# Transformer trunk on one core: opening stage, operand roles in gates and branches, and the planner's urgent calls

## The chip, the cores and the metric

The kernel runs on one core of a Trainium2 chip. A core has five engines that run side by side and meet at semaphores: TensorE (PE in the profile, with its weight loads shown as PEld) multiplies matrices into PSUM, VectorE (DVE) and ScalarE (ACT) work elementwise, GpSimd (POOL) does small side jobs, and SyncE (SP) issues the DMAs that bring data from memory. The metric is the time of one execution on the device in microseconds, the median of several runs.

## The reference

A sequence of 256 tokens of width 1024 passes two layers. Each layer takes shift, scale and gate rows from a vector c through a matrix of 1024 x 6144, normalises the tokens, mixes them by two attention branches that are gated and merged, and then applies a squared-ReLU MLP of width 4096. Cut to what matters:

```python
for l in range(DEPTH):
    ada = c_act @ w_ada[l] + b_ada[l]
    sh1, sc1, gt1, sh2, sc2, gt2 = [a[:, None, :] for a in jnp.split(ada, 6, axis=-1)]
    h = rms(x, g_mix[l]) * (1.0 + sc1) + sh1
    parts = jnp.split(h @ w_in[l], IN_SPLITS, axis=-1)
    y_a = gqa_attention(qa, ka, va) @ w_branch_a[l]
    y_b = dilated_attention(qs, kss, vs) @ w_branch_b[l]
    mixed = sigmoid(gate_a) * y_a + sigmoid(gate_b) * y_b
    x = x + gt1 * (mixed @ w_out[l])
    h2 = rms(x, g_mlp[l]) * (1.0 + sc2) + sh2
    x = x + gt2 * (jnp.square(jax.nn.relu(h2 @ w_ff1[l])) @ w_ff2[l])
```

All data is 32-bit float. Every weight is used once, so some 180 MB pass from memory to the core.

## The kernel before

**Numbers in two parts.** A product of two 32-bit matrices is made of three fast matmuls (`mm3`, line 682): each operand is split into a high part (a rounded copy) and a low part (the rest), and high x high, low x high and high x low are summed in PSUM. The weights come as tiles of 128 x 1024 (512 KB, `wr`); ACT writes the high part and DVE the low part (`split_next`, line 661). The activations are split the same way after each normalisation (`make_h`, line 731, into the tiles `hT`) and after each attention branch.

**Stages.** First c is made into `c_act`, spread over all partitions by small matmuls against columns of the identity. DVE multiplies each 128 x 1024 tile of the modulation matrix with it and sums along the row (`ada_tile`, line 597): 96 such tiles in all, 16 of which must be done before layer 0 has its first shift and scale. The opening loop (line 1320) takes one k block of 128 features at a time: two modulation tiles, the scaled and split activations of that block, and two weight tiles for four of the six QKV chunks. Ahead of it three matmuls on zeros (`WARM`) run. Then per layer follow the rest of the QKV chunks, the norm and rotary steps, attention a in four steps of head pairs and b in two, eight units of gate, four of branch a and four of branch b, the output product in two halves of 128 tokens, the residual and the norm for the MLP, and the MLP (`mlp`, line 1157). `CFG["seq0"]` and `CFG["seq1"]` give the order in which these pieces are written down: c a chunk, u and v a gate unit, a and b an attention step, w one modulation tile, y a piece of branch a.

**Which operand moves.** TensorE holds one operand of 128 x 128 (stationary) and passes the other through it (moving). In the QKV chunks, the output product and the second MLP product the activations are stationary and 512 weight columns move, so the result has tokens on the partitions. In `gates`, `ya` and the branch b loop the weights are stationary and the 256 tokens move (`wide`, line 1027), so the result has features on the partitions, as the output product needs its stationary operand `mT`:

```python
def wide(ps, i, wh, wl, xs, nk):
    o = ps[:, i * S : (i + 1) * S]
    for k in range(nk):
        mm3(o, wh[:, k, :], wl[:, k, :], *xs.parts(k, slice(0, S)), k == 0, k == nk - 1)
```

**The order of the work.** Nothing is issued as it is written. `Plan` (line 130) records each call with an estimated occupancy and latency (`cost`), links the calls by the data they share, gives each a due time from the place of the TensorE calls that need it (`due`), and plays the whole kernel against a clock (`run`): each engine takes the ready call that is due first, where its buffers fit (eight PSUM banks, seven short work tiles, fourteen large tiles, six raw weight tiles). `run` is repeated four times, each fed with the start times of the last, and the order of the shortest becomes the program: five queues, fixed before the chip starts. A call already lets an engine stay idle for a short time where another one due much earlier is nearly ready (`patience`). DMAs inside `plan.first()` go to the front of SP's queue.

**The point before the MLP.** The output product runs for tokens 0 to 127, then 128 to 255 (`mixer`, line 1081). After each half follow, on DVE, ACT and POOL, `residual`, `sum_sq`, the power on POOL, the scaling, eight transposes on TensorE and `make_h`. The first MLP unit (`ff1_first`, line 1168) needs the result of its half of the tokens.

Of the kernel before, what the change touches and what calls it, by code (L numbers as in the profile page):

```python
# [35 lines left out]
  dve_ss=0, hk=2,  # L36
# [5 lines left out]
WARM = 3  # L42
PSCALE = "aa"
PASSES = 4
HOLD = 400

# [83 lines left out]
class Plan:  # L130


    def __init__(self, tc, pools):
# [7 lines left out]
        self.soon = False  # L141
# [34 lines left out]
    @contextmanager  # L176
    def first(self):

        self.soon = True
        yield  # L180
        self.soon = False

# [34 lines left out]
    def record(self, e, op, a, k):  # L217
# [11 lines left out]
        o["occ"] += self.hold  # L229
        from_sbuf = all(z.space == bass.MemoryType.SB for z in ins)  # L230
# [4 lines left out]
    def cost(e, op, outs, ins, k):  # L235
# [3 lines left out]
        if e == "PE":  # L239
# [7 lines left out]
            occ = 232 if n > 256 else 119 if n > 128 else 109  # L247
# [3 lines left out]
        if e == "POOL":  # L251
            occ = 400 + 150 * n if k.get("op") == ALU.pow else 440 + 1.7 * n
            return occ, occ + 60
# [114 lines left out]
    def run(self, due):  # L368
# [8 lines left out]
        pipe = [1500.0]  # L377
# [11 lines left out]
        seen = dict.fromkeys(ORDERED)  # L389

        def fits(i):
# [14 lines left out]
            return True  # L406

# [5 lines left out]
        while count < n:  # L413
            moved = False
            for e in ORDERED:
# [15 lines left out]
                if pick is None and seen[e] == state[0]:  # L431
                    continue
                held = []
# [11 lines left out]
                if pick is not None and e != "SP" and not forced:  # L445

                    end = t + ops[pick]["occ"]
                    for r, j in w:
                        if r < end and due[j] < due[pick] - self.patience and (r - t) < 0.5 * ops[pick]["occ"] and fits(j):
                            held.append((due[pick], pick))  # L450
                            pick = None
                            break
                for h in held:
                    heapq.heappush(q, h)
# [23 lines left out]
                if e == "SP":  # L478
                    b = max(pipe[0], t + 2100.0) + o["lat"] / 380.0
                    pipe[0] = b  # L480
                    end = b + 1600.0
# [73 lines left out]
def encoder(ctx: ExitStack, tc: tile.TileContext, a: dict, out: bass.AP):  # L555
# [23 lines left out]
    def f32(t):  # L579
        return t.bitcast(F32)  # L580


    x = cp.tile([P, 2, D], F32, name="x")
    consts = cp.tile([P, P + 96 + 32 + 8], F32, name="consts")
    ident, small = consts[:, :P], consts[:, P:]
# [19 lines left out]
    def sh_sc(l, w, k0, k1):  # L605
# [5 lines left out]
        )  # L611

# [19 lines left out]
    def ada_jobs():  # L632
        for l in range(DEPTH):
            for w in range(2):
                shg[l, w] = tl("sbuf", [P, 2, KT], F32, "shg", 3, f"shg{l}{w}")
                for k in range(KT):
                    for s in range(2):
                        ada_tile(l, w, s, k, shg[l, w][:, s, k : k + 1])
                        if s == 1 and (l, w) == (0, 0):
                            sh_sc(0, 0, k, k + 1)  # L640
# [46 lines left out]

    ss_of = {}

    def sum_sq(l, w, t, c):  # L690
# [5 lines left out]
        if CFG["dve_ss"]:  # L696
# [4 lines left out]
    def rms_x(l, w, t):  # L701
# [5 lines left out]
        for g in range(2):  # L707
            xn = s2k(f"xn{l}{w}{t}{g}")
            dve.tensor_scalar(xn, x[:, t, g * 512 : (g + 1) * 512], r, None, op0=ALU.mult)
# [21 lines left out]
    def make_h(l, w, t, hT):  # L731
        v = shg[l, w]
        for g, ps in enumerate(rms_x(l, w, t)):
            h = s2k(f"h{l}{w}{t}{g}")
            for k in range(4):
                kk = 4 * g + k
                o, i = h[:, k * P : (k + 1) * P], ps[:, k * P : (k + 1) * P]
                if k < CFG["hk"]:
# [5 lines left out]
            dve.tensor_copy(hi, hv)  # L744
# [3 lines left out]
    def first_tables():  # L748
# [4 lines left out]
        gc = small[:, 128:136]  # L753
# [4 lines left out]
        for s in range(8):  # L758
            act.activation(dg[:, s * HD : (s + 1) * HD], e, AF.Copy, scale=gc[:, s : s + 1])
# [122 lines left out]
    def qkv_chunk(l, c, hT, T):  # L882
        pss = [pb(f"qkv{l}_{c}_{t}") for t in range(2)]
        for j in range(4):
            wh, wl = weights_k(2)
            for t in range(2):
                for k in range(2):
                    kk = 2 * j + k
                    lh, ll = hT.parts(kk, slice(t * P, (t + 1) * P))
                    mm3(pss[t], lh, ll, wh[:, k, :], wl[:, k, :], kk == 0, kk == KT - 1)  # L890
# [151 lines left out]
    def gates(l, hT, G, u, bank):  # L1042
        if u % 4 == 0:
# [411 lines left out]
```

## Time and profile before

| quantity | value |
| --- | --- |
| median of 3 runs | 755.84 us (755.43 to 757.5) |
| span of the profiled execution, first to last instruction | 754.0 us |
| TensorE busy, matmuls | 739.9 us in 4246 matmuls |
| VectorE, ScalarE, GpSimd busy | 595.4, 470.7, 70.2 us |
| read from memory | 178.66 MB, 238 GB/s over the span |
| mean granted TensorE clock | 0.995 |

The profile records one execution; its own time is its span with the start and end of a launch around it, which the records do not show, and the timed runs lie 1.4 to 3.5 us above the span. Almost every instruction carries line 551, at which the planner issues the calls, so its groups are to be told apart by the tiles they write and read: `ps<-w,hT` is a matmul that moves weights through stationary activations, `ps<-hT,w` one that moves activations, `ps<-consts,s2k` a transpose (the identity moves). A matmul's listed duration reaches beyond the start of the next one, since matmuls are pipelined; the time that one costs is the distance between the starts.

### The profile page before, as it was taken

The page shows a single profiled execution, that of the slowest core. Times are in us where ns is not written, and L with a number is a line of the kernel's source. Part 1 is how long each engine was busy: PE and PEld are TensorE (multiplying, and loading weights), DVE is VectorE, ACT ScalarE, POOL GpSimd, SP SyncE. Part 2 cuts the span into 40 slices and gives each one's busy share as a digit, 9 for nine tenths or more (in the row PEclk, how much of TensorE's full clock was granted, in tenths as well). Part 3 has the DMA queues.
Part 4 walks back from the last instruction along what each step waited for, and adds up shares of the span by engine and source line. Part 5 has one row for each costly group of instructions (what it writes and reads, how often), then busy time and mean ns, then how long its engine had stood idle before and what let it go on. Part 6 is the DMA issues. An engine that isn't in the chain of part 4 may idle for free.

```text
span 754.0 us, 11447 instructions
## 1 busy us (share of the span) xinstructions
PE 739.9 (98%) x4246; PEld 629.9 (84%) x4246; DVE 595.4 (79%) x905; ACT 470.7 (62%) x784; POOL 70.2 (9%) x60
## 2 busy tenths in 40 slices
PE   7999999999999999999999999999998999999997
PEld 4888898998788888888888788889987888888886
DVE  5999999889899989566499899778879976556633
ACT  8668469785558766655256557599535865555630
POOL 0007840000000060000002111000000000000000
PEclk9999999999999999999999999999999999999999
DMA  8996379976579999666145566966635986656201
GB/s 336 385 401 208 128 246 330 356 261 234 178 283 370 386 355 341 248 223 222 58 155 182 219 242 236 363 198 212 235 140 184 344 305 224 204 191 219 88 29 56
DMA packets 50391, 180.47 MB, mean 239 GB/s; under 512 B 5624, under 2 KB 6048, under 8 KB 50336
## 3 DMA queue, kind: packets, MB, share of 16 engines
q1 hardware_dynamic: 50336, 179.75, 66.6%
q8 instruction: 33, 0.54, 0.3%
q14 instruction: 22, 0.18, 0.1%
HBM read 178.66 MB, written 1.06 MB: 238 GB/s over the span
## 4 chain that ended last, share of the span: by engine, by line
PE 84%; DVE 7%; issue 4%; ACT 3%; DMA 1%; POOL 1%; SPq 0%; POOLq 0%; ACTq 0%; DVEq 0%
PE ps L551 84%; DVE s2k L551 4%; DVE w L551 2%; ACT s2k L551 2%; DVE rstd L551 1%; DMA x<-in_x 1%; ACT pr L551 1%; ACT w L551 0%; POOL s2k L551 0%; DVE x L551 0%; DVE hT L551 0%; ACT xT L551 0%; SPq L551 0%; POOL ss L551 0%; ACT c_act L551 0%
## 5 line engine op out<-in xcount | busy, mean ns | idle before, releaser
L551 DVE TENSOR_TENSOR w<-wr,w 128x1024 fp32r<-128x1024 f32 x236 | 288.0, 1238 | 61.0 <-ACT w L551 60.6
L551 ACT ACTIVATE w<-wr 128x1024 fp32r<-128x1024 f32 x236 | 245.6, 1058 | 87.2 <-PE ps L551 48.0
L551 PE MATMUL ps<-hT,w 128*128 128x256 f32 (+1 forms) x1664 | 263.8, 315 | 0.0
L551 PEld LDWEIGHTS ps<-hT,w 128*128 128x128 f32 x1664 | 234.4, 190 | 23.6 <-issue 2.6
L551 PE MATMUL ps<-w,r2k 128*128 128x512 f32 (+1 forms) x792 | 178.8, 385 | 0.0
L551 PEld LDWEIGHTS ps<-w,r2k 128*128 128x128 f32 x792 | 144.4, 188 | 30.1
L551 PE MATMUL ps<-w,hT 128*128 128x512 f32 x672 | 163.3, 399 | 5.0 <-DVE hT L551 2.7
L551 PEld LDWEIGHTS ps<-w,hT 128*128 128x128 f32 x672 | 126.2, 191 | 33.8 <-DVE hT L551 4.5
L551 DVE CUSTOM_DVE_ANT_0 s2k<-wr,c_act 128x1024 bf16<-128x1024 f32 x96 | 117.7, 1240 | 2.3 <-DMA wr<-in_w_ada 1.6
L551 ACT ACTIVATE s2k<-ps 128x512 f32<-128x512 f32 (+3 forms) x136 | 61.5, 479 | 64.0 <-PE ps L551 55.0
L551 PE MATMUL ps<-w,mT 128*128 128x512 f32 x192 | 44.5, 391 | 0.0
L551 ACT ACTIVATE s2k<-s2k 128x512 f32<-128x512 f32 (+1 forms) x62 | 38.3, 620 | 6.0 <-DVE s2k L551 5.2
L551 PEld LDWEIGHTS ps<-w,mT 128*128 128x128 f32 x192 | 35.8, 188 | 7.3
L551 POOL TENSOR_TENSOR rstd<-rstd,half 128x8 f32<-128x8 f32 (+1 forms) x20 | 35.7, 1795 | 61.7 <-DVE rstd L551 61.7
L551 DVE TENSOR_TENSOR s2k<-ps,s2k 128x256 f32<-128x256 f32 x56 | 23.6, 421 | 17.1 <-ACT s2k L551 17.1
L551 ACT ACTIVATE pr<-pr,st 128x256 f32<-128x256 f32 (+1 forms) x64 | 35.7, 614 | 0.6 <-DVE st L551 0.6
L551 POOL TENSOR_TENSOR ss<-ss,half 128x1 f32<-128x1 f32 x8 | 4.4, 554 | 312.2 <-DVE ss L551 312.2
L551 DVE TENSOR_TENSOR r2k<-s2k,r2k 128x512 fp32r<-128x512 f32 x28 | 19.6, 699 | 15.6 <-ACT r2k L551 15.6
L551 ACT ACTIVATE s2k<-x 128x512 bf16<-128x512 f32 x16 | 10.0, 627 | 31.2 <-DVE x L551 28.3
L551 DVE TENSOR_TENSOR s2k<-ps,gtb 128x512 f32<-128x512 f32 (+1 forms) x18 | 11.8, 659 | 20.5 <-PE ps L551 18.7
L551 PE MATMUL ps<-oa,w 128*128 128x256 f32 x192 | 26.1, 288 | 0.0
L551 PE MATMUL ps<-consts,s2k 128*128 128x128 f32 x148 | 22.6, 281 | 2.9 <-DVE s2k L551 2.4
(82 smaller groups left out, 498.1 us busy)
## 6 DMA issues: line engine op xcount, KB each, us to landing
wr<-in_w_ff SPq DMA_DIRECT2D x120, 512.0 KB, 5.2
wr<-in_w_ada SPq DMA_DIRECT2D x96, 512.0 KB, 5.3
wr<-in_w_gate SPq DMA_DIRECT2D x32, 512.0 KB, 5.1
wr<-in_w_qkv SPq DMA_DIRECT2D x24, 512.0 KB, 4.6
wr<-in_w_x SPq DMA_DIRECT2D x16, 512.0 KB, 3.2
wr<-in_w_out SPq DMA_DIRECT2D x16, 512.0 KB, 5.4
wr<-in_w_y SPq DMA_DIRECT2D x8, 512.0 KB, 5.5
wr<-in_w_ba SPq DMA_DIRECT2D x8, 512.0 KB, 4.9
```

Of the source, the lines that this page charges most:

```text
L551: getattr(self.real[o["e"]], o["op"])(*map(real, o["a"]), **{n: real(z) for n, z in o["k"].items()})
```

## The change

The diff does six things.

1. The opening. The constants come inside the two transfers of x and no longer in one of their own, the columns that spread c come with c, one warm-up matmul stays of three, the first two modulation tiles are asked for ahead of the table, sums of squares are shared by ACT and DVE, the diagonal for the rotary table is one DVE instruction, and the first k block's activations are made in halves.
2. `gates`, `ya` and branch b hold the activations and move 512 weight columns. Their results have tokens on the partitions, so branch b's merged result is transposed by TensorE before it is split into `mT`. A gate group takes two PSUM banks over four weight tiles.
3. `many` puts the products with the low part of the weights behind those with the high part, in the opening, the QKV chunks and the second MLP product; `ff1_first` puts those with the low part of the activations last.
4. `make_h` gives the first four feature blocks to ACT and the other four to DVE.
5. The planner's durations are new numbers, for matmuls, POOL and DMA.
6. Calls inside `plan.rush` are marked, on DVE and ACT, and before an engine takes an unmarked call the planner asks whether one of the next marked ones will be ready before that call ends (`called`); if so the engine is left idle.

```diff
-WARM = 3
+WARM = 1
+DEEP = 3
+URGE = 500.0
+GIVE = 0.75
...
+        o["rush"] = self.urgent and e in ("DVE", "ACT")
...
-            occ = 232 if n > 256 else 119 if n > 128 else 109
+            occ = 228.5 if n > 256 else 120.5 if n > 128 else 109
...
+        def called(e, pick, end):
+
+            q = rushed[e]
+            while q and start[q[0]] is not None:
+                q.pop(0)
+            for j in q[:4]:
+                if start[j] is None and due[j] < due[pick] - URGE:
+                    z = expect(j)
+                    if t + 1.0 < z < end and z - t < GIVE * (end - t):
+                        return True
+            return False
...
+                    if pick is not None and rushed[e] and not ops[pick]["rush"] and called(e, pick, end):
+                        held.append((due[pick], pick))
+                        pick = None
...
-                    b = max(pipe[0], t + 2100.0) + o["lat"] / 380.0
+                    quiet = t < 4000.0
+                    b = max(pipe[0], t + (1200.0 if quiet else 2100.0)) + o["lat"] / 400.0
...
+    def many(jobs):
+
+        for ps, lh, ll, rh, rl, start, stop in jobs:
+            pe.matmul(ps, lh, rh, start=start, stop=False)
+            pe.matmul(ps, ll, rh, start=False, stop=False)
+        for ps, lh, ll, rh, rl, start, stop in jobs:
+            pe.matmul(ps, lh, rl, start=False, stop=stop)
...
-                if k < CFG["hk"]:
+                if g == 0:
                     act.activation(o, i, AF.Identity, bias=v[:, 0, kk : kk + 1], scale=v[:, 1, kk : kk + 1])
...
-            dve.tensor_copy(hi, hv)
+            for k0 in (0, 2):
+                if g == 0:
+                    act.activation(hi[:, k0 : k0 + 2], hv[:, k0 : k0 + 2], AF.Copy)
+                elif k0 == 0:
+                    dve.tensor_copy(hi, hv)
...
-    def gates(l, hT, G, u, bank):
...
+    def gates(l, hT, G, pss, u):
+        g, part = divmod(u, 2)
...
+        if part == 0:
+            pss[:] = [pb(f"g{l}_{g}_{t}") for t in range(2)]
+        for j in (2 * part, 2 * part + 1):
+            wh, wl = weights_k(2)
+            for t in range(2):
+                for k in range(2):
+                    kk = 2 * j + k
+                    lh, ll = hT.parts(kk, slice(t * P, (t + 1) * P))
+                    mm3(pss[t], lh, ll, wh[:, k, :], wl[:, k, :], kk == 0, kk == KT - 1)
...
+        wb = [weights_k(2) for _ in range(2)]
+        for t in range(2):
+            ts = slice(t * P, (t + 1) * P)
+            for c in range(2):
...
+                m = s2k(f"yb{l}_{t}{c}s")
+                dve.tensor_tensor(m, ps, G[1][:, t, cs], op=ALU.mult)
+                dve.tensor_tensor(m, m, M[:, t, cs], op=ALU.add)
+                tp = pt(f"mT{l}_{t}{c}")
+                for k in range(4):
+                    pe.transpose(tp[:, k * P : (k + 1) * P], m[:, k * P : (k + 1) * P], ident)
...
+            with plan.rush(t == 1):
+                for c in range(2):
+                    residual(l, 0, t, c, ps[c])
+                    sum_sq(l, 1, t, c)
+                make_h(l, 1, t, h2)
...
+                for lows in range(2):
+                    for kk in range(KT):
+                        lh, ll = h2.parts(kk, slice(t * P, (t + 1) * P))
+                        wh, wl = (z[:, kk % 2, :] for z in ws[kk // 2])
+                        if lows:
+                            pe.matmul(ps, ll, wh, start=False, stop=kk == KT - 1)
+                        else:
+                            pe.matmul(ps, lh, wh, start=kk == 0, stop=False)
+                            pe.matmul(ps, lh, wl, start=False, stop=False)
...
     with plan.first():
-        sp.dma_start(c_row, a["c"])
-        sp.dma_start(x[:, 0, :], a["x"][0])
-        sp.dma_start(consts, a["consts"])
-        sp.dma_start(x[:, 1, :], a["x"][1])
+        sp.dma_start(c_in, a["c"])
+        for t in range(2):
+            sp.dma_start(xin[:, t, :], a["x"][t])
...
-                ps[:, k * P : (k + 1) * P], ident[:KT, kk : kk + 1].to_broadcast([KT, P]), c_row,
+                ps[:, k * P : (k + 1) * P], pick[:, kk : kk + 1].to_broadcast([KT, P]), c_row,
...
-            sum_sq(0, 0, t, c)
+            sum_sq(0, 0, t, c, c == 1)
...
-    tabs_of[0] = first_tables()
+    with plan.first():
+        ada(2)
+        tabs_of[0] = first_tables()
...
+        if k == 0:
+            for t in range(2):
+                ts = slice(t * P, (t + 1) * P)
+                dve.tensor_scalar(h[:, ts], xT[:, k, ts], v[:, 1, k : k + 1], v[:, 0, k : k + 1], op0=ALU.mult, op1=ALU.add)
+                act.activation(hi[:, ts], h[:, ts], AF.Copy)
+                dve.tensor_tensor(lo[:, ts], h[:, ts], f32(hi[:, ts]), op=ALU.subtract)
...
-        for pair in ((0, 1), (2, 5)):
+        for pair in ((0, 1), (2, 5)) if k < KT - 1 else ((2, 5), (0, 1)):
```

More of the change, by code (lines that the diff above doesn't have):

```diff
@@ L181, in first, with rush @@
         self.soon = False
+    @contextmanager
+    def rush(self, on=True):
+        self.urgent = on
+        yield
+        self.urgent = False
     @contextmanager
@@ L406, in fits, with expect @@
             return True
+        rushed = {e: [o["i"] for o in ops if o["e"] == e and o["rush"]] for e in ORDERED}
+        def expect(i, depth=0):
+            z = 0.0
+            for j, how in ops[i]["need"].items():
+                if start[j] is not None:
+                    b = start[j]
+                elif depth < DEEP:
+                    b = expect(j, depth + 1)
+                else:
+                    return 1e18
+                z = max(z, b + (ops[j]["lat"] if how == 2 else ops[j]["occ"]))
+                if z > 1e17:
+                    break
+            return max(z, t)
+        def called(e, pick, end):
[8 more added lines that the diff above has]
+            return False
         for o in ops:
@@ L430, in run @@
                     seen[e] = None
-                if pick is None and seen[e] == state[0]:
+                if pick is None and seen[e] == state[0] and e not in again:
                     continue
+                if e in again:
+                    again.remove(e)
                 held = []
@@ L1205, in ff1, with ff2_job @@
             return hid
+        def ff2_job(hid, w, j, i, t, c):
+            lh, ll = (z[:, (i % 2) * S + t * P : (i % 2) * S + (t + 1) * P] for z in hid[i // 2])
+            wh, wl = (z[:, c * 512 : (c + 1) * 512] for z in w)
+            last = 5 if (l, t, c) == (DEPTH - 1, 1, 1) else 7
+            return accs[2 * t + c], lh, ll, wh, wl, j == 0 and i == 0, j == last and i == 3
         def ff2_one(hid, w, j, i, t, c):
@@ L1222, in mlp @@
                     w = weights()
-                    for t in range(2):
-                        for c in range(2):
-                            ff2_one(hids[j - 1], w, j - 1, i, t, c)
+                    many([ff2_job(hids[j - 1], w, j - 1, i, t, c) for t in range(2) for c in range(2)])
         if l == 0:
@@ L1284, in encoder @@
         layer_weights(l)
[L1285 removed]
+    c_in = cp.tile([KT, P + KT], F32, name="c_in")
+    c_row, pick = c_in[:, :P], c_in[:, P:]
     with plan.first():
[L1287 to L1290 removed]
+        sp.dma_start(c_in, a["c"])
+        for t in range(2):
+            sp.dma_start(xin[:, t, :], a["x"][t])
     c_sig = s2k("c_sig")[:KT, :P]
```

180 lines of the change are left out of this document (103 added, 77 removed).

## The prediction

> **What bounds the kernel now.** I began with the page's busy shares and its chain of waits.
>
> ```profile
> PE 739.9 (98%) x4246; PEld 629.9 (84%) x4246; DVE 595.4 (79%) x905; ACT 470.7 (62%) x784; POOL 70.2 (9%) x60
> ...
> PE 84%; DVE 7%; issue 4%; ACT 3%; DMA 1%; POOL 1%; SPq 0%; POOLq 0%; ACTq 0%; DVEq 0%
> ```
>
> TensorE (PE) is busy nearly all the time and carries 84% of the chain. So the time is the opening, before PE has real work, plus the matmuls' own time, plus small gaps. The waits say what PE waited for (total us, times, longest us):
>
> ```profile
> PEld ps L551 <- DVE hT L551: 4.5, 5, 1.9
> ...
> PE ps L551 <- DVE hT L551: 2.7, 4, 1.4
> ...
> PE ps L551 <- ACT w L551: 0.2, 1, 0.2
> ```
>
> Its waits are for the transposed activations hT, hardly ever for a split weight w: 0.2 us in the whole run. A table of stretches (busy us of each engine, granted clock, DMA share, GB/s) shows what lies close behind:
>
> ```profile
> 15.90:19.30 3.40, 3.40 (x10) 2.48 (x9) 3.40 (x7) 3.40 (x6) 0.00 (x0) 0.50 1.02 404
> ...
> 20.00:60.00 40.00, 40.00 (x178) 33.12 (x177) 37.46 (x63) 25.29 (x34) 0.09 (x1) 1.00 1.02 391
> 60.00:220.00 160.00, 157.82 (x1089) 137.94 (x1088) 149.68 (x248) 112.29 (x213) 39.11 (x32) 1.00 0.69 238
> 300.00:380.00 80.00, 80.00 (x400) 67.47 (x399) 47.45 (x64) 42.41 (x63) 0.55 (x1) 1.00 0.54 184
> ...
> 575.70:579.10 3.40, 3.40 (x10) 2.82 (x11) 3.33 (x7) 1.83 (x4) 0.00 (x0) 0.50 0.05 19
> ```
>
> VectorE (DVE) has 37.46 of 40 us at 20 to 60 and 149.68 of 160 us at 60 to 220, about 94%, but only 59% at 300 to 380. DMA is full at 20 to 60. Twice PE had half its clock for 3.4 us, which costs 1.7 us each time.
>
> **The opening.** The rows, in order of time (start, length, engine):
>
> ```profile
> 1.45 4.93 PE L551 MATMUL ps<-warm 128*128 128x512 f32 x6 [1.45 <-DVE half L551]
> ...
> 2.59 0.28 DVE L551 SCALAR_TENSOR_TENSOR c_row<-s2k,c_row 8x128 f32<-8x128 f32 x1 [1.17 <-ACT s2k L551]
> ...
> 6.31 2.05 PE L551 MATMUL ps<-c_row,consts 8*128 8x128 f32 x16
> ...
> 7.41 0.63 ACT L551 ACTIVATE s2k<-x 128x512 bf16<-128x512 f32 x1 [0.82 <-DMA x<-in_x]
> ...
> 9.84 1.06 ACT L551 ACTIVATE c_act<-ps 128x512 f32<-128x512 f32 x2
> ...
> 10.93 1.23 DVE L551 CUSTOM_DVE_ANT_0 s2k<-wr,c_act 128x1024 bf16<-128x1024 f32 x1 [0.45 <-ACT c_act L551]
> ...
> 12.70 2.02 ACT L551 ACTIVATE w<-wr 128x1024 fp32r<-128x1024 f32 x2
> ...
> 14.60 0.62 ACT L551 ACTIVATE hT<-xT,shg 128x256 fp32r<-128x256 f32 x1
> ...
> 15.27 8.95 PE L551 MATMUL ps<-w,hT 128*128 128x512 f32 x31 [2.27 <-ACT hT L551]
> ```
>
> The row c_row is ready at 2.87, but PE is in the warm matmuls until 6.38, so it spreads c at 6.31 to 8.36; ScalarE (ACT) copies it at 9.84, after the squares of x and eight small diagonal copies; only then, at 10.93, does DVE start the first modulation sum. The change takes two of three warm matmuls away (1.64 us each, 4.93/3), brings the 8 by 8 picker with c so that the spreading no longer waits for the constants, and makes the diagonal one DVE instruction. Then c is spread from about 3.1. If that runs at half clock, 2.05 becomes 4.1 us and c_act is ready near 8 instead of 10.9. On SP's queue the order becomes c, x, x, two modulation tiles, rope table, weights: one issue fewer (the constants ride on x, same bytes), the table behind the tiles. In 0 to 12.5 us DMA moved about 300 GB/s (3.7 MB), and the first weight tile is complete after 3.0 MB, near 10.5 to 11.5, so it can be split by about 12.5. The two sums from 8.5 (1.23 us each), 0.3 us of small sums and the new quarter-size h take until about 11.8 to 12.5. PE then starts at about 12.8 instead of 15.27: -2.5 us. What could take it back is the pace after it. One k needs 24 matmuls of 0.227 us (row below), 5.45 us, against four tiles of 512 KB at 391 GB/s, 5.36 us. From the first weight 29 more tiles and the mask, 15.5 MB, take 39.6 us, to about 51.6; with the last split and matmuls the stage can end near 56.6, against 15.27 + 1.7 + 8 x 5.45 = 60.6 before. So DMA allows at most 4.0 us. Bounds: 0 (DVE, at 94%, gives nothing back) to -4.0. That the half-clock stretch stays (1.7 us) I keep; if fewer warm matmuls bring a second one, the gain falls to 0.8. DVE also gets two sums of squares and gives two scalings to ACT; both lie ahead of the modulation sums, in time that DVE waits.
>
> **Gates and branches with weights moving.** Before, weights stand in the array and 256 columns of activations move; after, activations stand and 512 weight columns move, so half as many matmuls of twice the width. Rows of unbroken stretches:
>
> ```profile
> 177.23 15.84 PE L551 MATMUL ps<-w,mT 128*128 128x512 f32 x69
> 192.91 1.03 PE L551 MATMUL ps<-consts,s2k 128*128 128x128 f32 x8
> 193.70 6.42 PE L551 MATMUL ps<-w,mT 128*128 128x512 f32 x27
> 199.95 4.70 PE L551 MATMUL ps<-w,hT 128*128 128x512 f32 x20
> ```
>
> ```profile
> 529.58 8.80 PE L551 MATMUL ps<-oa,w 128*128 128x256 f32 x72
> 538.22 5.82 PE L551 MATMUL ps<-ob,w 128*128 128x256 f32 x48
> 543.87 8.36 PE L551 MATMUL ps<-w,mT 128*128 128x512 f32 x36
> ```
>
> From start to start: (538.22 - 529.58)/72 = 120.0 ns at 256 columns, 5.65/48 = 117.7 for ob, and 15.68/69 = 227.2 at 512. The code counts 768 such matmuls in the gates of both layers, 192 in branch a, 96 in branch b: 960 x 120.0 + 96 x 117.7 ns = 126.5 us. After: 528 x 227.2 = 120.0. Saved 6.5 us. New are 32 transposes, four to a unit of branch b (two halves of tokens by two of columns, two layers): eight took 0.79 us (192.91 to 193.70), 99 ns each, and the stretch behind them took 6.25 us against 27 x 0.2272 = 6.13, so 0.12 for the switch: 8 x (4 x 0.099 + 0.12) = +4.1 us. Net -2.4 us. All of it is PE's own, with nothing to hide it; bounds -3.3 (no switch) to -1.5 (two).
>
> The Trainium skill, "TensorE: Matmul & The Clock Gate", section "Wait — 56ns, not 53.3ns?", speaks against this: it gives a fixed cost of only about 2.5 ns a matmul. By that an estimate of 528 pairs saves 1.3 us, and the transposes make the edit a loss of 2.8. The rows here give 2 x 120.0 - 227.2 = 12.8 ns, five times that; I go by the rows.
>
> The weights come in tiles of the same size, each for 12 matmuls of 227 ns (2.73 us) in place of 24 of 120 (2.88), so DMA and DVE get the same work in slightly less time. DVE has 10.3 us free of the 160 at 60 to 220, enough for the 1.2 us there. What changes is PSUM: a gate group holds two of eight banks over four tiles (10.9 us) where one bank was held over two (5.8). Nothing in this trace shows a shortage; the nearest is a gap while PE waited for a softmax:
>
> ```profile
> 96.31 0.33 PE L551 MATMUL ps<-consts,pr 128*128 128x128 f32 x1 [0.74 <-ACT pr L551]
> ```
>
> I charge one more such gap: +0.9 us with its small change, bounds -2.2 (all PE idle time of 60 to 220 gone, 160 - 157.82, by the better order) to the slow rival below.
>
> **The urgent calls.** Before the MLP the second half of the tokens must pass residual, norm, transposes and split while PE has little left:
>
> ```profile
> 565.60 2.35 DVE L551 TENSOR_TENSOR w<-wr,w 128x1024 fp32r<-128x1024 f32 x2
> ...
> 567.87 0.68 DVE L551 TENSOR_TENSOR s2k<-ps,gtb 128x512 f32<-128x512 f32 x1
> ...
> 569.19 1.22 DVE L551 TENSOR_TENSOR w<-wr,w 128x1024 fp32r<-128x1024 f32 x1
> ...
> 572.55 0.95 PE L551 MATMUL ps<-w,hT 128*128 128x512 f32 x3
> ...
> 574.95 0.50 PE L551 MATMUL ps<-w,hT 128*128 128x512 f32 x1 [1.45 <-DVE hT L551]
> ...
> 575.67 1.65 PE L551 MATMUL ps<-w,hT 128*128 128x512 f32 x3 [0.23 <-DVE hT L551]
> ```
>
> PE idles from 572.55 + 3 x 0.227 = 573.23 to 574.95 (1.72) and again 0.49 for the low half; then comes the half clock, 1.7 us. Two weight splits held DVE until 567.95; the output matmuls ended before the next ones began at 566.56, so the residual stood about 1.2 us behind splits nobody needed yet, and the split at 569.19 cost 0.3 more. The change reserves DVE and ACT for just these calls and computes both products with the high half first, which hides the second gap (0.49). Saved 1.2 + 0.3 + 0.49 = 2.0 of 2.2, and with a near-whole load the half clock should not follow. The moved copy of the first half costs ACT two instructions in place of one on DVE, inside ACT's idle time. I take -3.2 us (bounds 0 to -3.9). Queued behind the reserved engine are weight splits, which PE would wait for; it now waits 0.2 us for them. The same place in layer 0:
>
> ```profile
> 205.28 1.17 PE L551 MATMUL ps<-w,hT 128*128 128x512 f32 x4
> 207.21 0.49 PE L551 MATMUL ps<-w,hT 128*128 128x512 f32 x1 [0.77 <-DVE hT L551]
> 207.94 0.73 PE L551 MATMUL ps<-w,hT 128*128 128x512 f32 x2 [0.23 <-DVE hT L551]
> ```
>
> Gaps of 1.02 and 0.50 us, no half clock: -1.0 (bounds 0 to -1.5). The regrouped products in the QKV chunks and the MLP issue the same matmuls in another order, each with its own weight load: 0. The planner's new lengths only reorder; they sit in the +0.9.
>
> **Sum.** -2.5 - 2.4 - 3.2 - 1.0 + 0.9 = -8.2 us. The profiled span is 754.0, which makes 745.8; the median of the runs shown is 755.84, 1.8 us above that span, and nothing in the change touches what lies around it: 747.6 us.
>
> **Rivals.** (a) More: the opening reaches DMA's limit (-1.5 more) and the idle 2.2 us at 60 to 220 go as well in place of the +0.9: 747.6 - 1.5 - 3.1 = 743.0. For it: those gaps are waits for order, not for capacity. Against: DVE at 94%. (b) The reservation does not do what it says, because the planner's clock is not the chip's: the half clock and most of the gaps stay, +4.2: 751.8. For it: the delay was only 1.5 us long. Against: the high-first order works without it. (c) Halving the count saves nothing, each wide matmul taking as long as the two that it replaces: +6.5, 754.1; the cadence rows of mT, oa and ob speak against it. (By the section named above an estimate would stand 1.3 us below that.) (d) Slower: PSUM. In each of the 12 attention steps (four and two in each layer) PE must find other matmuls under the softmax:
>
> ```profile
> 484.24 2.34 ACT pr L551 x9
> ```
>
> If the banks held by gate groups leave it none for half of that, 1.17 us, the loss is 14.0 us: 761.6. It decides from 8.2/12 = 0.7 us a step. Against: gates are themselves the filler, and almost all of today's softmaxes are covered.
>
> **Chances.** Forecast 0.50, (a) 0.15, (b) 0.20, (c) 0.05, (d) 0.10. A change within 0.3% (2.3 us) can't be told from none, so (b) is mostly faster, and (c) is no change. Faster 0.82, same 0.08, slower 0.10. The range reaches from (a) to past (c): 742.5 to 755.0; the forecast's own is 744.5 to 750.5.
>
> **What would show it.** The first 512-wide matmul near 12.8; c_act copied before 9; 1056 matmuls of 256 columns replaced by 528 of 512, at 227 ns; 32 more transposes; no half-clock stretch near 570 and gaps under 0.7 us there; PE's idle time at 60 to 220 under 4 us. Wrong would be a start after 14.5, new PE waits for ACT pr, DVE w or a bank in the gate stages, or transposes that leave PE waiting for mT.

## The result

| | before | changed | ratio, 95% interval |
| --- | --- | --- | --- |
| first comparison | 755.84 us (754.96 to 757.68) | 752.28 us (751.13 to 754.12) | 0.9950 (0.9933 to 0.9967) |
| second comparison | 756.15 us (754.41 to 758.23) | 753.37 us (752.02 to 753.79) | 0.9955 (0.9938 to 0.9972) |
| span of the profiled execution | 754.0 us | 749.4 us, in the second comparison 752.0 us | |

The change makes the kernel 2.8 to 3.6 us faster, less than half of the 8.2 us that were forecast. The page of the changed kernel has 500 matmuls fewer and VectorE and ScalarE about as busy as before:

```profile
PE 738.6 (99%) x3746; PEld 600.4 (80%) x3746; DVE 594.1 (79%) x906; ACT 472.5 (63%) x786; POOL 69.2 (9%) x60
...
PE 83%; DVE 8%; ACT 4%; DMA 3%; issue 2%; POOL 1%; ACTq 0%; DVEq 0%
```

The chain of waits still runs 83% over TensorE; VectorE's share went from 7 to 8%, DMA's from 1 to 3%. TensorE's busy time fell by only 1.3 us where the span fell by 4.6: a matmul's record reaches past the start of the next one, so short waits vanish in it, and for costs I use distances between starts. The waits (us in all, times, longest) say where the new gaps lie:

```profile
PE ps L600 <- DVE w L600: 1.1, 3, 0.6
...
PE ps L600 <- ACT w L600: 0.4, 1, 0.4
PE ps L600 <- ACT hT L600: 0.2, 1, 0.2
```

Before, TensorE waited 2.7 us for DVE hT and next to nothing for a split weight. Now hT is down to 0.2 us, and 1.5 us are waits for a split weight, beside 1.4 us for DVE s2k (2.4 before). The stretches (busy us of PE, PEld, DVE, ACT and POOL, then the granted clock, the DMA share and GB/s):

```profile
15.27:18.70 3.43, 3.43 (x17) 2.84 (x16) 3.43 (x5) 3.43 (x6) 0.00 (x0) 1.00 1.02 391
60.00:220.00 160.00, 157.45 (x834) 122.20 (x834) 148.22 (x241) 112.31 (x216) 37.92 (x30) 1.00 0.69 240
571.00:578.00 7.00, 6.59 (x30) 4.85 (x30) 6.71 (x13) 5.23 (x12) 0.00 (x0) 1.00 0.44 129
```

The half-clock stretches of the opening and of layer 1's entry are gone: the clock is 1.00 where it was 0.50 at 15.9 and at 575.7. But at 60 to 220, where half as many matmuls of twice the width should have given TensorE time back, it idles 2.55 us where it idled 2.18.

**The timeline** of the changed kernel, first the opening, then two of the gaps in layer 0, unbroken rows of wide matmuls in layer 1, and the entry to layer 1's MLP (start, length, engine):

```profile
1.49 2.07 PE L600 MATMUL ps<-warm 128*128 128x512 f32 x2 [1.49 <-DVE warm L600]
...
3.49 3.78 PE L600 MATMUL ps<-c_in 8*128 8x128 f32 x16
...
5.60 0.60 ACT L600 ACTIVATE c_act<-ps 128x512 f32<-128x512 f32 x1
...
6.53 0.69 DVE L600 CUSTOM_DVE_ANT_0 s2k<-xin 128x512 bf16<-128x512 f32 x1 [0.75 <-DMA xin<-in_x]
...
7.30 0.60 ACT L600 ACTIVATE c_act<-ps 128x512 f32<-128x512 f32 x1 [1.11 <-PE ps L600]
...
8.54 0.16 DVE L600 SCALAR_TENSOR_TENSOR ss<-ss 128x1 f32<-128x1 f32 x1 [0.92 <-ACT s2k L600]
...
9.01 0.69 DVE L600 TENSOR_TENSOR s2k<-s2k,xin 128x512 f32<-128x512 f32 x1
...
9.62 1.22 DVE L600 CUSTOM_DVE_ANT_0 s2k<-wr,c_act 128x1024 bf16<-128x1024 f32 x1
...
11.36 2.08 PE L600 MATMUL ps<-s2k,s2k 64*128 64x128 f32 x8
...
13.37 0.89 PE L600 MATMUL ps<-xin,s2k 128*128 128x128 f32 x4
...
14.20 1.14 PE L600 MATMUL ps<-s2k,s2k 64*128 64x128 f32 x8
...
15.27 44.94 PE L600 MATMUL ps<-w,hT 128*128 128x512 f32 x194
...
121.67 1.22 DVE L600 CUSTOM_DVE_ANT_0 s2k<-wr,c_act 128x1024 bf16<-128x1024 f32 x1
...
122.82 1.22 DVE L600 TENSOR_TENSOR w<-wr,w 128x1024 fp32r<-128x1024 f32 x1
...
124.09 0.73 PE L600 MATMUL ps<-w,hT 128*128 128x512 f32 x2 [0.60 <-DVE w L600]
...
129.38 0.73 PE L600 MATMUL ps<-w,hT 128*128 128x512 f32 x2 [0.40 <-ACT w L600]
...
444.69 13.99 PE L600 MATMUL ps<-w,hT 128*128 128x512 f32 x61
458.57 0.66 PE L600 MATMUL ps<-xin,s2k 128*128 128x128 f32 x4
...
527.14 8.32 PE L600 MATMUL ps<-w,oa 128*128 128x512 f32 x36
535.30 3.67 PE L600 MATMUL ps<-w,ob 128*128 128x512 f32 x15
...
565.76 0.69 DVE L600 TENSOR_TENSOR s2k<-ps,gtb 128x512 f32<-128x512 f32 x1
...
570.75 1.18 PE L600 MATMUL ps<-w,hT 128*128 128x512 f32 x4
572.17 1.20 PE L600 MATMUL ps<-w,hT 128*128 128x512 f32 x4 [0.25 <-ACT hT L600]
```

c is spread and copied much earlier, but the first wide matmul starts at 15.27, as before (14.91 in the second profile). At 124.09 TensorE waits for a split weight that VectorE could begin only at 122.82, behind a modulation sum. At 572.17 the entry to the MLP has a gap of 0.25 us where there were 1.72 and 0.49.

**By stages.** Five events, taken from the timeline of each kernel, cut the span: the start of the 192nd wide matmul (end of the opening), of the last output matmul of layer 0 (`ps<-w,mT`), of the first matmul on `r2k` in layer 0 (the MLP has been entered), of the last output matmul of layer 1, and of its first matmul on `r2k`. Lengths in us:

| kernel | opening | L0 mixing | L0 entry to MLP | L0 MLP and L1 mixing | L1 entry to MLP | rest | span |
| --- | --- | --- | --- | --- | --- | --- | --- |
| before | 60.3 | 139.4 | 25.6 | 341.0 | 28.3 | 159.4 | 754.0 |
| changed | 59.4 | 141.7 | 24.7 | 339.4 | 25.0 | 159.2 | 749.4 |
| changed, second profile | 58.8 | 143.1 | 24.7 | 340.4 | 25.1 | 159.7 | 752.0 |
| old roles | 58.5 | 143.4 | 25.8 | 340.7 | 25.1 | 159.7 | 753.3 |
| new roles alone | 60.2 | 139.8 | 25.6 | 343.4 | 28.4 | 159.8 | 757.2 |
| no urgent marks | 59.3 | 142.9 | 24.7 | 339.9 | 25.1 | 159.7 | 751.6 |
| low part in old order | 59.5 | 142.4 | 25.9 | 340.7 | 26.4 | 159.8 | 754.6 |
| old lengths in the plan | 60.3 | 143.8 | 24.5 | 342.6 | 24.5 | 159.2 | 754.8 |
| late tables | 59.1 | 144.2 | 25.5 | 340.6 | 25.1 | 159.8 | 754.3 |
| scaling of three chunks on ACT | 58.7 | 140.5 | 25.3 | 339.7 | 25.0 | 159.2 | 748.5 |
| scaling of two chunks on ACT | 59.0 | 139.0 | 25.3 | 339.7 | 25.0 | 159.2 | 747.2 |
| the same, second profile | 59.3 | 139.8 | 25.5 | 340.0 | 25.1 | 159.8 | 749.3 |

The two profiles of the changed kernel show how far to trust such a table: a mixing stage repeats within 1.0 to 1.4 us, the two entries within 0.2. Each row is one execution, whose time lies up to 1.5 us from the median of its kernel (the changed kernel's first row 1.1 below it, old roles 1.5 below, low part in old order 1.3 above). Against before, the changed kernel gains 3.2 to 3.3 us at layer 1's entry, 0.9 at layer 0's, 0.6 to 1.6 in layer 1's mixing and 1.0 to 1.5 in the opening, and loses 2.3 to 3.7 us in layer 0's mixing. That loss is what the experiments had to explain.

### The profile page after: what moved, and what is told of

Its sections match the earlier page's. It is cut to its first block, busy times and chain, and to the rows that moved or that the text cites. A ratio compares the mean times of both kernels' runs of the same rounds, so it can differ in the third digit from the quotient of the medians.

```text
span 749.4 us, 10437 instructions
## 1 busy us (share of the span) xinstructions
PE 738.6 (99%) x3746; PEld 600.4 (80%) x3746; DVE 594.1 (79%) x906; ACT 472.5 (63%) x786; POOL 69.2 (9%) x60
## 4 chain that ended last, share of the span: by engine, by line
PE 83%; DVE 8%; ACT 4%; DMA 3%; issue 2%; POOL 1%; ACTq 0%; DVEq 0%
PE ps L600 83%; DVE s2k L600 3%; DVE w L600 2%; ACT s2k L600 2%; DMA wr<-in_w_ada 1%; DMA wr<-in_w_qkv 1%; ACT w L600 1%; DMA wr<-in_w_x 1%; DMA wr<-in_w_gate 1%; DVE rstd L600 1%; ACT pr L600 1%; POOL rstd L600 1%; DVE st L600 0%; DVE pr L600 0%; ACT G L600 0%
## 5 line engine op out<-in xcount | busy, mean ns | idle before, releaser
L600 PE MATMUL ps<-w,hT 128*128 128x512 f32 x1056 | 260.1, 397 | 1.8 <-DVE w L600 1.1
L600 PEld LDWEIGHTS ps<-w,hT 128*128 128x128 f32 x1056 | 193.9, 188 | 48.4 <-issue 4.5
L600 PE MATMUL ps<-hT,w 128*128 128x512 f32 (+1 forms) x896 | 159.5, 338 | 0.0
L600 PEld LDWEIGHTS ps<-hT,w 128*128 128x128 f32 x896 | 138.0, 188 | 20.2
L600 POOL TENSOR_TENSOR rstd<-rstd,half 128x8 f32<-128x8 f32 (+1 forms) x20 | 33.4, 1678 | 61.0 <-DVE rstd L600 60.9
L600 PEld LDWEIGHTS ps<-xin,s2k 128*128 128x128 f32 x180 | 22.0, 147 | 13.0 <-DVE s2k L600 3.9
L600 PE MATMUL ps<-xin,s2k 128*128 128x128 f32 x180 | 28.7, 288 | 3.2 <-DVE s2k L600 1.4
L600 ACT ACTIVATE s2k<-xin 128x512 bf16<-128x512 f32 x14 | 8.7, 624 | 28.0 <-DVE xin L600 25.9
```

Source lines behind the costliest of these rows:

```text
L600: getattr(self.real[o["e"]], o["op"])(*map(real, o["a"]), **{n: real(z) for n, z in o["k"].items()})
```

## The experiments

Theory S says that VectorE, and not TensorE, sets the length of layer 0 up to its last output matmul; what TensorE saves there, or how early it starts, cannot show. The rivals are that the new operand roles starve TensorE of PSUM banks or weights, that the urgent marks hold VectorE or ScalarE back, and that the plan is simply a fragile one (theory or rival O in the expectations). Each expectation names what it sets against each other; each run is timed against the kernel before on the same chip.

**Part 2 undone.** Gates and branches get their old roles, all else as changed:

```diff
-                    mm3(pss[t], lh, ll, wh[:, k, :], wl[:, k, :], kk == 0, kk == KT - 1)
...
+            wide(ps, i, wh, wl, hT, KT)
...
-                    mm3(yps[t], lh, ll, wh[:, k, :], wl[:, k, :], kk == 0, kk == 3)
...
+                wide(ps, i, wh[:, :, i * P : (i + 1) * P], wl[:, :, i * P : (i + 1) * P], T["oa"], 4)
```

> The changed kernel with part 2 undone: gates and both branches hold the weights again, no transposes of the merged result; all else as changed (752.28 us). Theory S (shared load): layer 0's mixing stage is held by VectorE and DMA, so the 1.2 us that TensorE saves there shows up as waits, and only layer 1's 1.2 us is worth anything: 753.5 us, and TensorE's new gaps at 120 to 140 us (2.7 us) go away. Theory O (order): the gaps are an accident of the planned order, the saving itself is whole: without both, 752.28 + 2.4 - 2.7 = 752.0 us. If the prediction's term was right and nothing else hangs on it: 754.7 us.

756.54 us, ratio 1.0004 (0.9986 to 1.0021): the whole gain is gone, and the time lies above all three that were expected. By stages, though, layer 0's mixing is as long with the old roles (143.4) as with the new ones (141.7 and 143.1). So the new roles did not lengthen it, and nothing shows that they shortened it. The profiled execution is the fastest of ten, so its row shows only a part of the loss.

**Part 2 alone**, put into the kernel before (the same edit, the other way round).

> The kernel before (755.84 us) with part 2 alone: weights move in gates and branches, 32 transposes more. By the cadences 2.4 us of TensorE time go. Theory S: layer 0's half of it is eaten by waits there, 754.6 us. Theory O: all of it shows, 753.4 us, unless this order has gaps of its own. Matmuls: 528 fewer, in both.

758.99 us, ratio 1.0026 (1.0008 to 1.0044): a small loss, where both theories expected a gain. Layer 0's mixing keeps its length (139.8 against 139.4). Layer 1's mixing, where the saving should show, is 2.4 us longer, with new gaps (TensorE idles 4.9 us in it in place of 2.3); one row of the timeline of this kernel:

```profile
510.36 1.21 PE L551 MATMUL ps<-w,oa 128*128 128x512 f32 x4 [0.80 <-DVE st L551]
```

A branch group starts late by 0.80 us, released when VectorE had read scores out of PSUM. That looks like the bank shortage of the prediction's rival (d), on a small scale. In the changed kernel, where the roles come with new lengths and order, this gap isn't there; with the old lengths in the plan it is back (0.80 us at 512.45). So the roles gain with the rest and lose alone; the two numbers don't add.

**The marks off.**

```diff
-        o["rush"] = self.urgent and e in ("DVE", "ACT")
+        o["rush"] = False
```

> The changed kernel with no call marked as urgent; all else as changed (752.28 us). If the reservation made the gain ahead of the MLP, the residual of the second half stands behind weight splits again: 1.5 us in layer 1 and, with the half-clock stretch, 3.2 us, and some 0.5 in layer 0: 756.0 us. Rival: the order of the low-part products and the shared split of the activations made it, the marking is worth nothing: 752.3 us, no half-clock stretch near 570 us.

753.40 us, ratio 0.9952 (0.9934 to 0.9970), the same as the changed kernel, with the same entries to the MLP (24.7 and 25.1 us). The reservation is worth nothing, and does no harm.

**The low part in its old order** at the entry to the MLP:

```diff
-                        if lows:
-                            pe.matmul(ps, ll, wh, start=False, stop=kk == KT - 1)
-                        else:
-                            pe.matmul(ps, lh, wh, start=kk == 0, stop=False)
-                            pe.matmul(ps, lh, wl, start=False, stop=False)
...
+                    mm3(ps, lh, ll, wh, wl, kk == 0, kk == KT - 1)
```

> The changed kernel with the first MLP unit's products in the old order (high, low, cross per block); the marks stay. If putting the low-part products last made the gain ahead of the MLP: layer 1's gap and half-clock stretch come back, 3.3 us, and 1.0 us in layer 0: 756.6 us. If the shared split of the activations in the norm step made it: 752.3 us.

755.06 us, ratio 0.9987 (0.9972 to 1.0001). Layer 1's entry is 1.3 to 1.5 us longer, layer 0's 1.2. Its timeline:

```profile
575.33 0.50 PE L600 MATMUL ps<-w,hT 128*128 128x512 f32 x1 [0.18 <-ACT hT L600]
576.70 0.66 PE L600 MATMUL ps<-xin,s2k 128*128 128x128 f32 x4 [0.87 <-ACT s2k L600]
577.73 2.60 PE L600 MATMUL ps<-w,hT 128*128 128x512 f32 x10 [0.37 <-DVE hT L600]
```

Three gaps come back (0.18, 0.87, 0.37), and no half clock after them. So of the 3.3 us at layer 1's entry about 1.4 is this order; that the half clock stays away (1.7 us) hangs on neither the order nor the marks by itself; both undone together weren't run. The time lies between the two expected (756.6 and 752.3).

**Late tables.** The products for the rotary table and the last transposes of x are put behind the first twelve wide matmuls:

```diff
-        tabs_of[0] = first_tables()
+        tab_parts = first_tables()
+        tabs_of[0] = tab_parts[0]
...
+            if k == 0 and pair == (0, 1):
+                x_copy(*next(x_parts))
+                first_tables_rest(*tab_parts)
```

> The changed kernel with TensorE's rotary table products and the last four transposes of x placed behind the first 12 wide matmuls instead of ahead of them. Theory: TensorE's own queue held the start at 15.27 us while the first operands were ready at 13.7: the start moves to about 13.8 us and the whole to 750.8 us. Rival: VectorE and DMA pace the opening (VectorE 94% busy, DMA full), the start moves but the 192nd wide matmul stays at 59.4 us: 752.3 us.

755.03 us, ratio 0.9976 (0.9959 to 0.9992). TensorE starts 1.2 to 1.6 us earlier, and nothing comes of it; by the medians the kernel is even 1.6 us slower than the one without marks (753.40) on the same chip, and slower than either expectation:

```profile
13.70 3.29 PE L600 MATMUL ps<-w,hT 128*128 128x512 f32 x13
16.92 1.14 PE L600 MATMUL ps<-s2k,s2k 64*128 64x128 f32 x8
```

The opening ends at 59.1, within the spread of the changed kernel (58.8 to 59.4), since the work put off is done in it all the same, and the last output matmul of layer 0 comes at 203.3, with 185.1 us of VectorE's work ahead of it. The start of the first wide matmul, which I had taken as the measure of the opening, doesn't set its end.

**VectorE's load, less and more.** In the first of these two runs seven of the eight modulation tiles of layer 0's first gate are left out, and the gate is zero there, so that part of layer 0 isn't computed; in the second eight sums are done twice:

```diff
-                    ada_tile(l, w, 2, k, gcol[l, w][:, k : k + 1])
+                    if (l, w) != (0, 0) or k == 0:
+                        ada_tile(l, w, 2, k, gcol[l, w][:, k : k + 1])
```

> The changed kernel without seven of the eight modulation tiles of layer 0's first gate row (their columns are set to zero, so layer 0's gate is left out in part): 7 x 1.31 us of VectorE work and 3.7 MB of transfers fewer in layer 0's mixing stage, no TensorE work touched. Theory S (VectorE holds this stage): the stage from the 192nd wide matmul to the last output matmul, 141.7 us, shrinks until TensorE's own gaps there (6.3 us of 60 to 160) are down to some 2, to 137 us; 748 us in all. Rival O (gaps are accidents of the order): 141 to 142 us and about 752 us.

```diff
-        dve.tensor_tensor_reduce(junk, raw, c_act, 0.5, 0.0, ALU.mult, ALU.add, col)
+        for _ in range(2 if (l, w, s) == (0, 0, 2) else 1):
+            dve.tensor_tensor_reduce(junk, raw, c_act, 0.5, 0.0, ALU.mult, ALU.add, col)
```

> The changed kernel with each of those eight modulation sums done twice into the same column: 8 x 1.31 = 10.5 us more of VectorE work in layer 0's mixing stage, no transfer and no TensorE work more. Theory S: nearly all of it shows, the stage grows from 141.7 to about 150 us, 761 us in all. Rival O, with VectorE's 10.6 idle us in that stage to take it: at most 3 us more. If transfers and not VectorE held the stage: no change.

746.37 us, ratio 0.9886 (0.9844 to 0.9929), and 762.84 us, ratio 1.0104 (1.0057 to 1.0151). These two speak for theory S. The stretch from the start to layer 0's last output matmul in one row each (length, then busy us of PE, PEld, DVE): the kernel before,

```profile
0.00:199.72 199.72, 194.63 (x1232) 165.32 (x1233) 180.35 (x303) 142.23 (x261) 39.95 (x37) 0.99 0.78 283
```

the changed kernel,

```profile
0.00:201.06 201.06, 196.10 (x980) 151.10 (x981) 181.79 (x309) 140.99 (x254) 40.88 (x37) 1.00 0.78 281
```

the new roles alone,

```profile
0.00:200.06 200.06, 194.75 (x985) 150.35 (x985) 179.87 (x303) 142.09 (x260) 38.20 (x37) 0.99 0.77 282
```

fewer sums,

```profile
0.00:194.02 194.02, 191.69 (x980) 151.66 (x981) 174.71 (x298) 139.29 (x254) 38.16 (x37) 1.00 0.76 275
```

and more sums:

```profile
0.00:212.33 212.33, 198.85 (x981) 153.03 (x982) 190.08 (x323) 140.75 (x253) 39.75 (x37) 0.98 0.73 264
```

VectorE's busy time goes from 174.7 over 180.4 and 181.8 to 190.1, the end of the stage from 194.0 over 199.7 and 201.1 to 212.3. The difference between the two, VectorE's idle time, is 19.3, 19.4, 19.3 and 22.2 us. TensorE's 250 matmuls fewer (1232 to 980 records) move nothing. Fewer sums also leave out 3.7 MB of DMA (7 x 512 KB), so that run alone would not decide; but the doubled sums, which move no byte more, lengthen the stretch by 11.3 us for 8.3 us more of VectorE's work. The 3.0 us beyond that come with half the clock from 88.1 to 94.9 us, behind a wait of TensorE for VectorE (2.93 us, to 89.06); 6.8 us at half the clock cost TensorE at most 3.4, so at least 7.9 of the 11.3 us go with VectorE's work. Over all fourteen traces VectorE's idle time up to layer 0's last output matmul lies between 17.8 and 22.2 us, while the end itself moves by 18.3.

**The plan with the lengths of before.**

```diff
-            occ = 228.5 if n > 256 else 120.5 if n > 128 else 109
+            occ = 232 if n > 256 else 119 if n > 128 else 109
...
-                    quiet = t < 4000.0
-                    b = max(pipe[0], t + (1200.0 if quiet else 2100.0)) + o["lat"] / 400.0
+                    b = max(pipe[0], t + 2100.0) + o["lat"] / 380.0
```

> The changed kernel planned with the old durations for matmuls, POOL and DMA. If the new durations are what let layer 0's stage run late, its 141.7 us fall to about 139.4, the value of the kernel before: 750 us. If VectorE's load holds it whatever the plan: 141 to 143 us, 752 to 753 us.

755.35 us, ratio 0.9993 (0.9977 to 1.0008), later than either expectation. The opening is 0.9 to 1.4 us longer and layer 1's mixing 2.1 to 3.1; the entries are as short as in the changed kernel (24.5 us each). Nearly the whole gain hangs on the new lengths, as it did on the roles and, for three quarters of it, on the low part's order.

**VectorE relieved.** If S holds, moving work from VectorE to ScalarE in layer 0 must give time back. The scaling of the rotated heads by 1/rms goes to ScalarE, head by head, first in three chunks, then in two:

```diff
-        dve.tensor_tensor(v3(t1), v3(t1), r[:, :, None].to_broadcast([P, nh, HD]), op=ALU.mult)
+        if l == 0 and c in (2, 3, 4):
+            for h in range(nh):
+                act.activation(v3(t1)[:, h, :], v3(t1)[:, h, :], AF.Copy, scale=r[:, h : h + 1])
+        else:
+            dve.tensor_tensor(v3(t1), v3(t1), r[:, :, None].to_broadcast([P, nh, HD]), op=ALU.mult)
```

> The changed kernel with one load taken from VectorE in layer 0: in the QKV chunks 2, 3 and 4 the scaling of the rotated heads by 1/rms (6 instructions of 0.81 us on VectorE) is done by ScalarE, head by head (48 instructions of about 0.24 us, 11.6 us, in a stage in which ScalarE idles about 38 us). Same products, same matmuls. Theory S (layer 0's mixing stage is as long as VectorE's work in it plus about 10 us): VectorE's busy time there falls by 4.9 us, the stage from 141.7 to about 137, and the time by 3 to 4.9 us, to about 748. Rival O (the gain was lost because the order that the planner finds is a fragile one, and each other plan ends 2 to 4 us later, whatever VectorE has to do): 752 to 756. Rival A (ScalarE, which all softmaxes need, becomes what the heads wait for): slower than the changed kernel, with new waits of TensorE for ACT s2k near 70 to 110.

> As the run before, for the chunks 3 and 4 alone (4 instructions, VectorE -3.2 us, ScalarE +7.7 us). Theory S: the stage 2 to 3.2 us shorter than in the changed kernel, the time about 749.5, between the changed kernel and the run before. Rival O: 752 to 756, without an order between the two.

Three chunks: 750.56 us, ratio 0.9932 (0.9912 to 0.9951). Two chunks: 749.42 us, ratio 0.9918 (0.9896 to 0.9939). S had expected about 748 and 749.5. The larger move fell short and gives no more than the smaller one: 1.1 us less, though the ranges of the two overlap (749.55 to 751.78 and 749.03 to 750.80). The timeline of the larger shows what it met:

```profile
113.82 0.33 PE L600 MATMUL ps<-xin,s2k 128*128 128x128 f32 x1 [1.74 <-ACT s2k L600]
```

TensorE waits 1.74 us for heads that ScalarE is still scaling: rival A of the expectation, beside S and not in its place. The two profiles with two chunks have no wait for scaled heads over 0.2 us.

**Both on one chip.** The changed kernel and the one with two chunks moved, both as they stand above, side by side:

> The changed kernel as it is, beside the next run on the same chip. It shows how far two profiles of one program lie apart (the stage ends, which the comparison of the runs rests on, should agree within about 1 us) and gives the difference to the next run without another chip between them. Theory S: 752 to 753, with the last output matmul of layer 0 within 1 us of 201.1. If two profiles of it lie 2 us or more apart there, the stage ends of the other runs can't be read to less than that.

> The kernel with ScalarE scaling the heads of chunks 3 and 4 in layer 0 once more, beside the changed kernel. Theory S: 2 to 3.2 us faster than the changed kernel of the same job, the last output matmul of layer 0 near 198. If the first result was a matter of the run or the chip, within 1 us of it.

753.37 us (752.02 to 753.79) and 750.76 us (749.33 to 751.63), ratios to before 0.9955 (0.9938 to 0.9972) and 0.9926 (0.9910 to 0.9941). The two don't overlap: 2.6 us. The stretch to layer 0's last output matmul, of the changed kernel here,

```profile
0.00:201.93 201.93, 196.12 (x981) 150.60 (x981) 181.75 (x309) 140.61 (x254) 40.87 (x37) 1.00 0.76 280
```

and with two chunks moved:

```profile
0.00:199.00 199.00, 194.48 (x980) 151.09 (x981) 179.93 (x305) 148.16 (x286) 40.81 (x37) 1.00 0.78 284
```

VectorE does 1.8 us less and idles 1.1 us less, the stage ends 2.9 us earlier, and 2.6 of these reach the end of the kernel. (3.3 us of scaling were moved; the 58 weight splits ahead of that point took 73.1 us in place of 71.9, for a reason not traced.) It is the fastest complete kernel of the study, by its two comparisons 5.4 and 6.9 us faster than before.

## Why the prediction was right or wrong

The direction was right and 752.28 lies in the range of 742.5 to 755.0, but the size was wrong: -3.6 us for -8.2. The sum by its terms, against the stages (first and second profile of the changed kernel):

| term | forecast | measured |
| --- | --- | --- |
| opening | -2.5 | -1.0, -1.5, and then taken back |
| roles, layer 0 (half of -2.4), and one more gap (+0.9) | -0.3 | +2.3, +3.7 |
| entry to the MLP, layer 0 | -1.0 | -0.9, -0.9 |
| roles, layer 1 | -1.2 | -1.6, -0.6 |
| entry to the MLP, layer 1 | -3.2 | -3.3, -3.2 |
| rest | 0 | -0.2, +0.3 |
| sum | -8.2 | -4.7, -2.1 |

Everything behind layer 0's mixing came out as forecast to within 0.6 us. All that is missing was lost before layer 0's last output matmul: -2.8 was forecast to there, +1.3 and +2.2 were measured.

**The step that failed** is "PE then starts at about 12.8 instead of 15.27: -2.5 us" in the opening and "All of it is PE's own, with nothing to hide it" in the roles. The prediction had read VectorE at 94% in both stretches and named the bound that follows, 0 for the opening ("DVE, at 94%, gives nothing back"), and then took the sum of TensorE's terms all the same. In layer 0 TensorE is busy 98% of the time and is still not the bound: it works at the pace at which VectorE splits weights and sums modulation tiles. Its recorded busy time up to layer 0's last output matmul even rose, from 194.6 to 196.1 us, with less to do by the cadences, so the 98% seems to hold waits that the records don't show. The 10.3 us in which VectorE idles at 60 to 220 I had read as room ("enough for the 1.2 us there"). They weren't room: from the start to layer 0's last output matmul VectorE idled 19 to 20 us in the kernel before, in the changed one and with 5.6 us less work than before, and 22 us with 9.7 us more, where room would have shrunk. So the end of layer 0's mixing should have been forecast from VectorE's list of work, 1.4 us longer than before (181.8 against 180.4 busy us), not from TensorE's. The roles have no part in that: alone they leave VectorE at 179.9, and without them it has 182.3. The largest items are in the opening: two sums of squares (1.39 us) came to VectorE and two scalings (0.97) left it, which the prediction had put at nothing as "time that DVE waits". One more weight split ahead of that point (58 in place of 57) adds little, 71.9 us for all of them against 71.6.

**Opening.** Right: c_act copied before 9 (5.60 and 7.30), the half-clock price (3.78 us for the 16 small matmuls in place of 2.05), no change in DMA. Wrong: the first modulation sum at 9.62 instead of 8.5, because the sums of squares and the scaling that "lie ahead of the modulation sums, in time that DVE waits" hold VectorE from 6.53 on, 0.92 us of it in a wait for ScalarE's share of the squares; and the first wide matmul at 15.27 instead of 12.8, in part because the transposes and table products ahead of it ran slowly (8 in 2.08 us at 11.36, 8 in 1.14 at 14.20); put behind it, they let it start at 13.70. The half-clock stretch, which I kept, went (clock 1.00 at 15.27 to 18.70), and its 1.7 us are about the 1.0 to 1.5 measured. But that it made this gain isn't shown: with the old lengths in the plan there is no half clock at that place either, and the opening is 60.3 us, as before. A slip in the bound changes nothing here: a first weight at 10.5 to 11.5 and 39.6 us of DMA make 50.1 to 51.1, not 51.6.

**Roles.** The cadence held: (458.57 - 444.69)/61 = 227.5 ns and (535.30 - 527.14)/36 = 226.7 for 512 columns, against 227.2 forecast. Rival (c), that halving the count saves nothing, is refuted. The fixed part of a matmul comes out as 2 x 120.0 - 227.5 = 12.5 ns. The same rows speak against the Trainium skill, "TensorE: Matmul & The Clock Gate", section "Wait — 56ns, not 53.3ns?": the about 2.5 ns a matmul that it gives are a fifth of that. The stage that holds layer 1's mixing became 0.6 to 1.6 us shorter, about the 1.2 forecast, but that the roles made it isn't shown: undone they cost 0.3 to 1.3 us there, and alone they made it 2.4 us longer. In layer 0 no saving shows.

**The gap term** (+0.9) stood for PSUM. The waits that came were the ones listed as a sign of error, for split weights (1.1 us for DVE w, 0.4 for ACT w): mostly VectorE's work again. Waits of a branch group that look like a bank's came in other runs only: in the roles alone, with late tables, with old lengths and with two chunks scaled on ScalarE, 0.5 to 1.3 us each. The sign I had named, TensorE's idle time under 4 us at 60 to 220, is there with 2.55 and shows nothing, because a stage can be longer with no more idle time in a window of fixed length.

**The urgent calls** were right in size, partly by luck, and wrong in cause. I gave the reservation 1.5 us and the half clock's absence to it as well; with 0.49 for the order the parts make 3.7, of which I took 3.2 without a reason. Without the marks both entries are the same. Measured, the order of the low part is worth 1.3 to 1.5 us (0.49 forecast) and the absent half clock 1.7; the residual now starts 0.57 us after the start of the last output matmul, with the marks or without, where it stood behind two splits and started 1.53 us after it. Whether it is the activations made in two halves on two engines (part 4) or only another outcome of the plan that brings that about wasn't isolated.

**Rivals.** (b), that the reservation doesn't do what it says, gave 751.8 and came nearest in time, but by another way: the reservation does nothing, yet its gaps closed. (a) and (d) didn't come.

**Open.** VectorE's 19 to 20 idle us in layer 0 weren't traced to one cause; the largest named share is its wait for ScalarE's high part of a weight split (5.4 us before, 6.1 in the changed kernel). And the parts don't add: undoing the roles, the lengths or the low part's order costs most of the gain each, by stages mainly in layer 1's mixing and the entries. That the planned order is re-made for each of them is the likely reason, but it was only argued.

## What to carry to other kernels

An engine at 98% need not be the bound of its stage: an engine at 94% that feeds it can set the pace, and its last few idle per cent need not be room for more work. Forecast each stage from the work list of every engine that is nearly full, and test the bound by adding and taking work on one engine alone; here the stage followed VectorE's work within 3 us over a range of 15. And measure a stage by when it ends, not by when its first instruction starts.

## What the runs showed of the hardware

**The clock in the opening.** With three warm matmuls (4.93 us) the 16 spreading matmuls took 2.05 us; with one (2.07 us) they took 3.78, and small matmuls stayed at about half rate until 13.9, though TensorE was in matmuls from 3.49 to 7.27: eight of 64 x 128 started 251 ns apart ((13.37 - 11.36)/8) and the next eight, from 14.20, 134 ns apart ((15.27 - 14.20)/8). The column of the granted clock shows 1.00 there for want of a record: in the traces the clock's records begin, at 1.00, only at 13.91 us here and at 5.68 us in the kernel before, so the half rate is read from the distances, and the first record and the change of pace fall together. The Trainium skill, "TensorE: Matmul & The Clock Gate", section "What's actually happening", says that the array starts at half rate and is released by one busy window of about 3.4 us; the half rate at the start agrees, but here 3.8 us of matmuls with 8 rows didn't release it.

**Idle time ahead of a half clock.** Before, 1.72 and 0.49 us of idle time shortly after each other were followed by half the clock from 575.70 to 579.10. With the old lengths in the plan it came at 70.24 to 73.65, with five waits of 0.16 to 0.67 us from 63.1 on, and with more sums at 88.07 to 94.90, in a wait of 2.93 us. It didn't come after 0.25 us in the changed kernel, after 0.18, 0.87 and 0.37 us with the low part in its old order, nor after single waits of 1.74 us (three chunks) and 2.06 us (more sums, at 112.26). So the length of one wait doesn't tell. The changes of the granted clock in these traces lie whole multiples of 3.41 us apart (10.24, 3.41, 556.37 and 3.41 in the kernel before).

**Two profiles of one program** differ by 0.9 us at 200 us and by 2.6 us at the end, while the two entries to the MLP repeat within 0.2 us.
